# One run of column-half products per expert, then the scatter and both pairs of transposes

## The chip, the cores and the metric

The kernel runs on one core of a Trainium2 chip (trn2). The metric is the device time of one execution in microseconds; the number given for a kernel is the median of its runs.

## The reference

Two transformer layers over 256 tokens of width 1024. Layer 0 mixes with a gated linear attention, layer 1 with a differential attention; each is followed by a hierarchical mixture of experts, and the change touches only that mixture, which runs once per layer:

```python
def hier_moe(x, w_group, b_group, w_router, b_router, w_gate, w_up, w_down):
    ...                                  # a group, then 2 of its 4 experts for each token
    for e in range(MOE_EXPERTS):         # 16
        hdn = jax.nn.silu(t @ w_gate[e]) * (t @ w_up[e])      # 1024 -> 512
        y = y + combine[:, e:e + 1] * (hdn @ w_down[e])       # 512 -> 1024
    return y.reshape(B, S, D)
```

All arithmetic is float32.

## The kernel before

Each token takes two experts, so an expert sees about 32 of the 256 tokens. The kernel gives each expert 64 places. It gathers the tokens of four experts at a time into `xg` by products with one-hot matrices (line 548), and adds an expert's result back by a product with the transposed one-hot matrix `st`, which is called the scatter (line 664). Experts with more than 64 tokens get a further block; layer 1 always runs one such block as a 17th pass of the loop, so the two loops together have 33 passes.

With 64 tokens a product fills only half of the columns of TensorE's array. So the products with the weights are issued as pairs, one on each column half, that run at the same time; the profile marks them with the tile 128\*64. The gather, the scatter and the transposes use the whole array (128\*128). Of one expert:

- `gu_part` (line 604): tokens times gate and up weights, in four parts (0,), (1,), (2,) and (3,) with one weight tile each, on column halves, into a bank `pB`.
- `act_part`: ScalarE takes the silu of the gate half into `sl` (line 611), VectorE multiplies it with the up half into `hd` (line 613).
- `tr_part`: TensorE transposes `hd` in two pieces (line 620, whole array), VectorE copies the result to `ht` (line 623).
- `down_part`: `ht` times the down weights, on column halves (line 632). ScalarE and VectorE scale the result by the combine weights `wst` and split it in two numbers (lines 640 and 641).
- `s_prep`: VectorE builds the weighted one-hot matrix `ohw` (line 586), TensorE transposes it in two pieces (line 589, whole array), VectorE makes `st` of the result (line 591), and ScalarE sums the rows of the same bank into `wst` with its output thrown away into `jk` (line 594).
- `scatter`: four products on the whole array into the four banks of `y` (line 664).

The loop is pipelined by one expert: in the pass of expert e, the down products and the scatter are those of expert e - 1. Within a pass TensorE's order before is gu (0), transposes of `hd`, gu (1), down, transposes of `ohw`, gu (2, 3), scatter. Each engine works through its own queue in the order in which the scheduler of the kernel's framework put it. `issue_after` pins instructions of an engine behind a given one of the same engine.

The buffers `sl` and `jk` have the same tag with one buffer, so a silu and a row sum never hold it together:

```python
jk = mp.tile([128, S], F32, tag="sl", bufs=1, name=nm("jk"))   # s_prep, line 593
...
sl = mp.tile([128, fw], F32, tag="sl", bufs=1, name=nm("sl"))  # act_part, line 610
```

The weights (6 MB an expert) come through a ring of 16 tiles of 1 MB, filled by one DMA queue.

Of the kernel before, what the change touches and what calls it, by code (L numbers as in the profile page):

```python
# [22 lines left out]
E = 16  # L23
# [20 lines left out]
def body(ctx, tc, x, w_in, wa_out, kv_w, wq, wb_out, wg, wu, wd, gate2, rows, rtab, lng, lnb, cblob, pblob, onehot, out):  # L44
    nc = tc.nc
    pe, act, dve, pool, sp = nc.tensor, nc.scalar, nc.vector, nc.gpsimd, nc.sync
# [17 lines left out]
    def pB():  # L64
        return psum.tile([128, 512], F32, tag="B", bufs=2, name=nm("pB"))
# [14 lines left out]
    ident = ident_r.bitcast(F32)  # L80
# [383 lines left out]
    def moe(layer, M, lg, rstd, nd, fold, side=None):  # L464
        with tc.tile_pool(name=f"moe{layer}", bufs=1) as mp:
# [42 lines left out]
            OH = {}  # L508
# [73 lines left out]
            def s_prep(ohv, m, c_):  # L582

                w2 = mp.tile([128, 2, 2, m], F32, tag="ohw", bufs=2, name=nm("ohw"))
                for b in range(2):
                    dve.tensor_scalar(w2[:, b], ohv(b).unsqueeze(1).broadcast_to([128, 2, m]), c_[:, b:b + 1], None, op0=ALU.mult)
                p = pC()
                for b in range(2):
                    pe.transpose(p[0:2 * m, b * 128:b * 128 + 128], w2[:, b].rearrange("p d s -> p (d s)"), ident)  # L589
                st = mp.tile([128, S], F32R, tag="st", bufs=2, name=nm("st"))[0:2 * m]  # L590
                dve.tensor_scalar(st, p[0:2 * m, 0:256], 0.0, None, op0=ALU.is_gt)  # L591
                ws = sm([128, 1], "wst")
                jk = mp.tile([128, S], F32, tag="sl", bufs=1, name=nm("jk"))
                act.activation(jk[0:2 * m], p[0:2 * m, 0:256], AF.Copy, accum_out=ws[0:2 * m])
                return st, ws

            def gu_part(ws, js, xg, p, nt):
                m, fw = 128 // nt, FF // nt
# [17 lines left out]
            def tr_part(h, nt, filler=0):  # L616
                n = 4 // nt
                pt = pC()
                for c in range(n):
                    mm = pe.transpose(pt[:, c * 128:c * 128 + 128], h[:, c * 128:c * 128 + 128], ident)  # L620
                warm(filler, mm)
                ht = mp.tile([128, n, 128], F32, tag="ht", bufs=2, name=nm("ht"))
                dve.tensor_copy(ht, pt[:, 0:n * 128].rearrange("p (c t) -> p c t", c=n))  # L623
                return ht

            def down_part(wd_, ht, ws, nt, filler=0):

                m, n, w = 128 // nt, 4 // nt, D // nt
                p = [pB(), pC()]
                for q in range(4):  # L630
                    for c in range(nt):
                        mm = pe.matmul(p[2 * c // nt][c * m:c * m + m, 0:w], ht[:, q % n, (q // n) * m:(q // n) * m + m], wd_[q // 2][:, q % 2, c * w:c * w + w],  # L632
                                  start=q == 0, stop=q == 3)
                warm(filler, mm)
                o = [mp.tile([128, 512], F32R, tag="o", bufs=2, name=nm("o"))[0:2 * m] for _ in range(2)]
                for c in range(nt):
                    h, f = 2 * c // nt, slice(c * w % 512, c * w % 512 + w)
                    src, a = p[h][c * m:c * m + m, 0:w], h * m
                    hi, lo = o[h][a:a + m, f], o[h][m - a:2 * m - a, f]
                    act.activation(hi, src, AF.Copy, scale=ws[a:a + m, 0:1])  # L640
                    dve.scalar_tensor_tensor(lo, src, ws[a:a + m, 0:1], hi, op0=ALU.mult, op1=ALU.subtract)
                return o

            def down_last(wd_, ht, ws):

# [15 lines left out]
            def scatter(st, o, last, cols_first=False):  # L661
                for i in range(4):
                        b, c = (i % 2, i // 2) if cols_first else (i // 2, i % 2)
                        pe.matmul(y[b][c], st[:, b * 128:b * 128 + 128], o[c], start=False, stop=last, skip_group_check=True)  # L664

            def blocks():

# [62 lines left out]
            def overflow(left, base, rev):  # L730

                ei, q, cwx = pick(left, base, rev)
                ws, wdn = reload(ei, lambda j: spare_tile(1 + j % 2, [128, 2048], F32, nm("W")), pool, mybir.EngineType.Pool)
                oh = mp.tile([128, 2, 64], F32, tag="ohw", bufs=2, name=nm("ohx"))
                for b in range(2):
                    dve.tensor_scalar(oh[:, b], iota, q[:, b:b + 1], None, op0=ALU.is_equal)
                st, wsx = s_prep(lambda b: oh[:, b], 64, cwx)
                p = pC()
                pv = p.rearrange("p (k s) -> p k s", k=KC)
                for k in range(KC):  # L740
                    for b in range(2):
                        pe.matmul(pv[:, k], xa[:, b, k * 128:k * 128 + 128], oh[:, b], start=b == 0, stop=b == 1)
                xg = mp.tile([128, KC, 64], F32, tag="o", bufs=2, name=nm("xgx"))
                gv, bv = (pb[:, c:c + KC].unsqueeze(2).broadcast_to([128, KC, 64]) for c in (gcol, bcol))
                dve.tensor_mul(xg, pv, gv)
                dve.tensor_add(xg, xg, bv)
                p = pB()
                gu_part(ws, range(4), lambda k: xg[:, k], p, 2)
                ht = tr_part(act_part(p, 2), 2)
                scatter(st, down_part(wdn, ht, wsx, 2), True)  # L750

            xs0 = [split_x(k, dve) for k in range(4)]
            act.activation(sm([128, 2], "warm"), xs0[3][:, 0, 0, 0:2], AF.Exp, scale=0.0)
# [5 lines left out]
            for e in range(E + layer):  # L759
                g = min(e // 4, 3)  # L760
                if e in (4, 8, 12):
                    with after(held[e][1]):
                        one_hot(g)
                    gather_group(g, held[e][0])
                sl4 = slice((e - 4 * g) * 64, (e - 4 * g) * 64 + 64)
                xg = lambda k, t=xg_tiles[g if e < E else 4], s=sl4 if e < E else slice(0, 64): t[:, k, s]
                p = pB()
                mm = gu_part(M[e][0], (0,), xg, p, 2)
                if prev is not None:
                    with tc.issue_after(getattr(mm, "ins", mm)):  # L770
                        ht = tr_part(prev[0], 2)
                mm = gu_part(M[e][0], (1,), xg, p, 2)
                if prev is not None:
                    with tc.issue_after(getattr(mm, "ins", mm)):
                        o = down_part(M[e - 1][1], ht, prev[2], 2)
                sp_ = s_prep(lambda b: OH[g][:, b, e - 4 * g], 64, cw[:, :, e] if e < E else extra[2])
                gu_part(M[e][0], (2, 3), xg, p, 2)
                if prev is not None:
                    scatter(prev[1], o, False)
                h = act_part(p, 2)  # L780
                if e == 1:
                    over = blocks()
                    extra = over[1]
                    if layer:
                        M.append(reload(extra[0], lambda j: ring_slot(), sp, mybir.EngineType.SP))
                    nblocks = nc.values_load(over[0][0:1, 0:1], min_val=0, max_val=7, skip_runtime_bounds_check_because="512 tokens of experts, 65 or more for a block")
                prev = (h, *sp_)
                if e in (1, 5, 9):
                    held[e + 3] = anchor[0], anchor[1]
                if e == 5:  # L790
                    xr = spare_tile(2, [128, 2, D], F32, "xr")
                    for _ in residual(2 * layer, xr):
                        pass

                    for b in range(2):
                        for h in range(2):
                            v = xr[:, b, h * 512:h * 512 + 512]
                            hi, lo = (mp.tile([128, 512], F32R, tag="o", bufs=2, name=nm("res")) for _ in range(2))
                            act.activation(hi, v, AF.Copy)
                            dve.tensor_sub(lo, v, hi)  # L800
                            for a in (hi, lo):
                                pe.matmul(y[b][h], ident_r, a, start=False, stop=False, skip_group_check=True)
                if e == 9 and layer:
                    gb = spare_tile(0, [128, 2, 2, 512], F32, "gb")
                    for i in range(2):
                        for h in range(2):
                            act.activation(gb[:, i, h], bcast_row(8 * i + 4 * layer + 2 + h, pC), AF.Copy)
                if e == 9 and side:
                    side()
            o = down_last(M[-1][1], tr_part(prev[0], 2), prev[2])  # L810
            scatter(prev[1], o, True, True)
            with tc.If(nblocks > 0, label=f"over{layer}"):
                with tc.For_i(0, nblocks, 1):
# [163 lines left out]
    prev = None  # L977
# [231 lines left out]
```

## Time and profile before

| | us |
|---|---|
| median of 3 runs (780.3 to 781.99) | 780.58 |
| the profiled execution, its own time | 782.23 |
| the profiled execution, span from first to last instruction | 780.6 |
| TensorE busy in the span | 751.2 |

The span is what the trace shows; the profiled execution's own time is 1.6 us more, and is itself 1.65 us above the median. In a trace, a product of a 32-bit operand appears as two matmul records, so `gu_part` of one weight tile, 4 products, is 8 records. The granted TensorE clock is given as a share of full speed: 1.00 is 2.4 GHz and 0.50 is 1.2 GHz.

### The profile page before, as it was taken

To read this page: it belongs to the slowest core of one execution; us is meant where nothing else is said; L and a number is where in the kernel's file an instruction comes from. 1 tells how busy PE (TensorE), PEld (TensorE's weight loads), DVE (VectorE), ACT (ScalarE), POOL (GpSimd) and SP (SyncE) were. 2 spreads that over 40 slices of the span, in tenths; PEclk is the share of its full clock that TensorE was granted. 3 is DMA by queue.
4 is the path that set the end of the run, shared out by engine and by line. 5 is a ranking of instruction groups with operands and counts; after the bars stand their busy time and mean duration, and the time that the engine had idled before them with its cause. 6 is when DMAs were issued, how large, how long until landed. Compare 5 with 4: busy or idle time off the path is not lost. (4 is left out here: it accounts for less than half of the span.)

```text
span 780.6 us, 10650 instructions
## 1 busy us (share of the span) xinstructions
PE 751.2 (96%) x3762; PEld 404.2 (52%) x3762; DVE 362.7 (46%) x959; ACT 299.7 (38%) x655; POOL 8.4 (1%) x20
## 2 busy tenths in 40 slices
PE   7999999999999999999899999999999999999993
PEld 5887677534333433433689887763343243343331
DVE  3645576533363422422567777773344432332225
ACT  4444466523222331312557666562132232242123
POOL 1100000000000000000000000000000000000000
PEclk9999999999999999999999999999999999999997
DMA  7999448499999999999998336619999999999941
GB/s 217 312 385 392 168 164 295 152 381 397 394 386 393 392 395 396 393 392 367 290 363 314 144 111 215 216 56 370 393 395 395 394 391 390 397 394 392 391 168 56
DMA packets 131792, 246.02 MB, mean 315 GB/s; under 512 B 7916, under 2 KB 38101, under 8 KB 131734
## 3 DMA queue, kind: packets, MB, share of 16 engines
q1 hardware_dynamic: 131270, 244.68, 86.3%
q8 instruction: 32, 0.52, 0.3%
q10 hardware_dynamic: 432, 0.59, 0.2%
q14 instruction: 26, 0.21, 0.1%
q0 software_dynamic: 32, 0.01, 0.0%
HBM read 244.19 MB, written 1.06 MB: 314 GB/s over the span
## 5 line engine op out<-in xcount | busy, mean ns | idle before, releaser
L604 PE MATMUL pB<-W,xg 128*64 128x512 f32 x1056 | 258.7, 602 | 0.0
L604 PEld LDWEIGHTS pB<-W,xg 128*64 128x64 f32 x1056 | 69.1, 136 | 117.1 <-issue 110.2
L632 PE MATMUL pC<-W,ht 128*64 128x512 f32 x248 | 112.9, 594 | 0.0
L632 PE MATMUL pB<-W,ht 128*64 128x512 f32 x248 | 112.9, 594 | 0.0
L640 ACT ACTIVATE o<-pB,wst 64x512 fp32r<-64x512 f32 x31 | 21.1, 682 | 221.8 <-PE pC L632 208.4
L591 DVE TENSOR_SCALAR st<-pC 128x256 fp32r<-128x256 f32 x33 | 14.0, 425 | 155.2 <-PE pC L589 155.2
L119 DVE TENSOR_TENSOR lo<-W,hi 128x512 fp32r<-128x512 f32 x96 | 66.3, 696 | 39.9 <-PE pA L128 26.4
L118 ACT ACTIVATE hi<-W 128x512 fp32r<-128x512 f32 x96 | 59.5, 630 | 51.4 <-PE pA L129 29.8
L632 PEld LDWEIGHTS pB<-W,ht 128*64 128x64 f32 x248 | 33.3, 137 | 62.8 <-issue 61.2
L664 PE MATMUL pA<-o,st 128*128 128x512 f32 x132 | 40.2, 423 | 2.7 <-DVE o L658 2.1
L623 DVE COPY ht<-pC 128x256 f32<-128x256 f32 x33 | 14.0, 424 | 60.8 <-PE pC L620 60.7
L613 DVE TENSOR_TENSOR hd<-sl,pB 128x256 f32<-128x256 f32 x33 | 13.9, 422 | 56.7 <-ACT sl L611 56.6
L548 PE MATMUL pC<-OH,xs 128*128 128x256 f32 (+1 forms) x256 | 36.4, 292 | 3.1 <-ACT xg L555 1.9
L664 PEld LDWEIGHTS pA<-o,st 128*128 128x128 f32 x132 | 21.9, 188 | 33.5 <-issue 23.5
L548 PEld LDWEIGHTS pC<-OH,xs 128*128 128x128 f32 x256 | 32.8, 190 | 10.9 <-ACT xs L529 6.1
L127 PE MATMUL pA<-x1Thi,hi 128*128 128x256 f32 x128 | 36.5, 288 | 0.0
L632 PEld LDWEIGHTS pC<-W,ht 128*64 128x64 f32 x248 | 33.3, 137 | 6.1 <-issue 5.1
L128 PE MATMUL pA<-x1Tlo,hi 128*128 128x256 f32 x128 | 36.2, 285 | 0.0
L129 PE MATMUL pA<-x1Thi,lo 128*128 128x256 f32 x128 | 35.6, 288 | 0.0
L611 ACT ACTIVATE sl<-pB 128x256 f32<-128x256 f32 x33 | 12.7, 385 | 58.6 <-PE pB L604 58.4
L128 PE MATMUL pA<-lo,xThi 128*128 128x384 f32 (+1 forms) x96 | 35.0, 364 | 0.0
L129 PE MATMUL pA<-hi,xTlo 128*128 128x384 f32 (+1 forms) x96 | 34.7, 361 | 0.0
(340 smaller groups left out, 1148.1 us busy)
## 6 DMA issues: line engine op xcount, KB each, us to landing
W<-in_moe_w_gate_dram SPq DMA_DIRECT2D x132, 512.0 KB, 10.9
W<-in_moe_w_up_dram SPq DMA_DIRECT2D x132, 512.0 KB, 10.8
W<-in_moe_w_down_dram SPq DMA_DIRECT2D x66, 1024.0 KB, 12.0
W<-in_a_w_in_dram SPq DMA_DIRECT2D x16, 256.0 KB, 6.3
W<-in_a_w_in_dram SPq DMA_DIRECT2D x4, 1024.0 KB, 13.3
W<-in_a_w_out_dram SPq DMA_DIRECT2D x4, 1024.0 KB, 14.9
W<-in_kv_w_dram SPq DMA_DIRECT2D x4, 1024.0 KB, 8.9
W<-in_b_w_q_dram SPq DMA_DIRECT2D x16, 256.0 KB, 5.4
```

The lines of the kernel that those rows point to most:

```text
L118: act.activation(hi, src, AF.Copy)
L119: dve.tensor_sub(lo, src, hi)
L127: pe.matmul(o, l[0], r[0], start=first, stop=False, skip_group_check=skip)
L128: pe.matmul(o, l[0], r[1], start=False, stop=False, skip_group_check=skip)
L129: pe.matmul(o, l[1], r[0], start=False, stop=last, skip_group_check=skip)
L548: pe.matmul(o, xs[k][:, q // 2, q % 2], OH[g][:, q % 2].rearrange("p e s -> p (e s)"), start=q == 0, stop=q == 3)
L591: dve.tensor_scalar(st, p[0:2 * m, 0:256], 0.0, None, op0=ALU.is_gt)
L604: mm = pe.matmul(p[c * m:c * m + m, 0:2 * fw].rearrange("p (g f) -> p g f", g=2), xg(k), w[:, :, kk, c * fw:c * fw + fw], start=k == 0, st ...
L623: dve.tensor_copy(ht, pt[:, 0:n * 128].rearrange("p (c t) -> p c t", c=n))
L632: mm = pe.matmul(p[2 * c // nt][c * m:c * m + m, 0:w], ht[:, q % n, (q // n) * m:(q // n) * m + m], wd_[q // 2][:, q % 2, c * w:c * w + w] ...
L640: act.activation(hi, src, AF.Copy, scale=ws[a:a + m, 0:1])
L664: pe.matmul(y[b][c], st[:, b * 128:b * 128 + 128], o[c], start=False, stop=last, skip_group_check=True)
```

## The change

A pass now has on TensorE: gu (0), down products of expert e - 1, gu (1, 2, 3), scatter of expert e - 1, transposes of `ohw` of expert e, transposes of `hd` of expert e. All column-half products of a pass form one run, and all whole-array work stands behind it. The transposes of `hd` thereby move from the pass of e + 1 to the end of the pass of e. Chains of `issue_after` pin this order on TensorE. Nothing is computed differently.

```diff
                 p = pB()
-                mm = gu_part(M[e][0], (0,), xg, p, 2)
-                if prev is not None:
-                    with tc.issue_after(getattr(mm, "ins", mm)):
-                        ht = tr_part(prev[0], 2)
-                mm = gu_part(M[e][0], (1,), xg, p, 2)
+                with after(prev and prev[4]):
+                    mm = gu_part(M[e][0], (0,), xg, p, 2)
                 if prev is not None:
-                    with tc.issue_after(getattr(mm, "ins", mm)):
-                        o = down_part(M[e - 1][1], ht, prev[2], 2)
-                sp_ = s_prep(lambda b: OH[g][:, b, e - 4 * g], 64, cw[:, :, e] if e < E else extra[2])
-                gu_part(M[e][0], (2, 3), xg, p, 2)
-                if prev is not None:
-                    scatter(prev[1], o, False)
-                h = act_part(p, 2)
+                    with after(mm):
+                        o, mm = down_part(M[e - 1][1], ht, prev[2], 2)
+                with after(mm):
+                    mm = gu_part(M[e][0], (1, 2, 3), xg, p, 2)
+                with after(mm):
+                    if prev is not None:
+                        mm = scatter(prev[1], o, False)
+                    with after(mm):
+                        sp_ = s_prep(lambda b: OH[g][:, b, e - 4 * g], 64, cw[:, :, e] if e < E else extra[2])
+                    h = act_part(p, 2)
+                    with after(sp_[2]):
+                        ht, mm = tr_part(h, 2)
...
-                prev = (h, *sp_)
+                prev = (h, *sp_, mm)
...
-            o = down_last(M[-1][1], tr_part(prev[0], 2), prev[2])
+            o = down_last(M[-1][1], ht, prev[2])
```

The other lines of the diff only hand the last TensorE instruction of `s_prep`, `tr_part`, `down_part` and `scatter` back to the caller.

TensorE's queue before, in the pass of expert 2 of layer 0 (down products, of which 2 of 8 rows are shown, and the scatter are expert 1's; `W` is a weight tile, `hd_1878` expert 1's, `ohw_1932` expert 2's):

```order
L604 MATMUL pB_1902<-W_200,xg_1719 64x512 x4
L620 MATMUL pC_1907<-ident_r,hd_1878 128x128 x2
L604 MATMUL pB_1902<-W_203,xg_1719 64x512 x4
L632 MATMUL pB_1916<-W_196,ht_1910 64x512
L632 MATMUL pC_1917<-W_196,ht_1910 64x512
...
L589 MATMUL pC_1935<-ident_r,ohw_1932 128x128 x2
L604 MATMUL pB_1902<-W_206,xg_1719 64x512 x4
L604 MATMUL pB_1902<-W_209,xg_1719 64x512 x4
L664 MATMUL pA_1658<-o_1926,st_1859 128x512
```

TensorE's queue of the change in the same pass (`hd_1957` and `ohw_1944` are expert 2's):

```order
L604 MATMUL pB_1907<-W_200,xg_1719 64x512 x4
L632 MATMUL pB_1912<-W_196,ht_1883 64x512
L632 MATMUL pC_1913<-W_196,ht_1883 64x512
...
L604 MATMUL pB_1907<-W_203,xg_1719 64x512 x4
L604 MATMUL pB_1907<-W_206,xg_1719 64x512 x4
L604 MATMUL pB_1907<-W_209,xg_1719 64x512 x4
L664 MATMUL pA_1658<-o_1922,st_1871 128x512
...
L589 MATMUL pC_1947<-ident_r,ohw_1944 128x128 x2
L620 MATMUL pC_1959<-ident_r,hd_1957 128x128 x2
```

The transposes of `ohw` moved from before gu (2, 3) to behind the scatter, and the transposes of `hd` directly behind them; 31 of the 33 passes have these neighbours, and the first pass of each layer, which has no scatter, has line 589 and line 620 behind its gu (3).

ScalarE's queue before, in the passes of experts 2 and 3 of layer 0 (lines 640: results of the down products; `jk`: row sum; `sl`: silu):

```order
L640 ACTIVATE o_1926<-pB_1916,wst_1861 64x512
L640 ACTIVATE o_1927<-pC_1917,wst_1861 64x512
L594 ACTIVATE jk_1941,wst_1940<-pC_1935 128x256
L611 ACTIVATE sl_1955<-pB_1902 128x256
L640 ACTIVATE o_1983<-pB_1973,wst_1940 64x512
```

ScalarE's queue of the change at the same place:

```order
L640 ACTIVATE o_1922<-pB_1912,wst_1873 64x512
L640 ACTIVATE o_1923<-pC_1913,wst_1873 64x512
L594 ACTIVATE jk_1953,wst_1952<-pC_1947 128x256
L611 ACTIVATE sl_1955<-pB_1907 128x256
L640 ACTIVATE o_1979<-pB_1969,wst_1952 64x512
```

Nothing moved on ScalarE: the row sum of expert 2 (line 594) stands ahead of its silu (line 611) both times. What changed is the place on TensorE of the transposes `pC_1935` or `pC_1947` that the row sum reads.

## Rows read from the trace of the kernel before

**Rows 1.** The page's busy times: engine, busy us (share of span), instructions.
```profile
PE 751.2 (96%) x3762; PEld 404.2 (52%) x3762; DVE 362.7 (46%) x959; ACT 299.7 (38%) x655; POOL 8.4 (1%) x20
```

**Rows 2.** TensorE's waits: us in total, times, longest us (longest wait for weights).
```profile
PEld pB L604 <- DMA W<-in_moe_w_gate_dram: 2.9, 9, 0.8
```

**Rows 3.** Timeline of TensorE, one pass of layer 1: start us, us, instruction.
```profile
552.17 3.65 PE L604 MATMUL pB<-W,xg 128*64 128x512 f32 x16
555.76 1.20 PE L664 MATMUL pA<-o,st 128*128 128x512 f32 x4
556.88 1.94 PE L604 MATMUL pB<-W,xg 128*64 128x512 f32 x8
558.75 0.44 PE L620 MATMUL pC<-ident_r,hd 128*128 128x128 f32 x2
559.12 1.94 PE L604 MATMUL pB<-W,xg 128*64 128x512 f32 x8
560.88 0.59 PE L632 MATMUL pB<-W,ht 128*64 128x512 f32 x1
...
564.42 0.44 PE L589 MATMUL pC<-ident_r,ohw 128*128 128x128 f32 x2
564.79 3.65 PE L604 MATMUL pB<-W,xg 128*64 128x512 f32 x16
```

**Rows 4.** Timeline of TensorE: a scatter followed by whole-array products.
```profile
191.87 1.20 PE L664 MATMUL pA<-o,st 128*128 128x512 f32 x4
192.91 2.06 PE L548 MATMUL pC<-OH,xs 128*128 128x256 f32 x16
```

**Rows 5.** Timeline, layer 0: the first transposes of `ohw` and what follows.
```profile
151.24 0.44 PE L589 MATMUL pC<-ident_r,ohw 128*128 128x128 f32 x2
151.72 0.42 DVE L591 TENSOR_SCALAR st<-pC 128x256 fp32r<-128x256 f32 x1 [1.08 <-PE pC L589]
152.18 0.38 ACT L594 ACTIVATE jk<-pC 128x256 f32<-128x256 f32 x1 [2.38 <-DVE st L591]
152.46 0.19 ACT L594 ACTIVATION_READ_ACCUMULATOR jk<-pC 128x1 f32 x1
```

**Rows 6.** Timeline: the one pass where silu follows the row sum at once.
```profile
241.59 0.38 ACT L594 ACTIVATE jk<-pC 128x256 f32<-128x256 f32 x1
...
242.22 0.39 ACT L611 ACTIVATE sl<-pB 128x256 f32<-128x256 f32 x1
```

**Rows 7.** Timeline: the end of layer 1's loop, from its last scatter in the loop.
```profile
760.81 1.20 PE L664 MATMUL pA<-o,st 128*128 128x512 f32 x4
760.99 0.39 ACT L611 ACTIVATE sl<-pB 128x256 f32<-128x256 f32 x1 [2.01 <-PE pB L604]
761.41 0.42 DVE L613 TENSOR_TENSOR hd<-sl,pB 128x256 f32<-128x256 f32 x1 [2.08 <-ACT sl L611]
761.88 0.44 PE L620 MATMUL pC<-ident_r,hd 128*128 128x128 f32 x2
...
762.84 0.43 PE L652 MATMUL pB<-W,ht 128*64 128x256 f32 x1 [0.52 <-DVE ht L623]
```

**Rows 8.** Line 611: duration ns min/median/max, first and last start us.
```profile
L611 ACT ACT_TABLE_LOAD  x2: 1283/1283/1283, 155.4 to 531.9; - x2
```

**Rows 9.** Windows: us; busy us (count) by engine; granted clock, DMA share, GB/s.
```profile
29.30:33.00 3.70, 3.70 (x22) 2.67 (x20) 2.56 (x9) 1.82 (x4) 1.45 (x2) 1.00 1.14 317
33.00:36.40 3.40, 3.40 (x12) 2.94 (x11) 2.20 (x5) 0.63 (x1) 0.00 (x0) 0.50 1.14 319
...
376.00:380.00 4.00, 2.84 (x11) 2.04 (x12) 2.72 (x5) 3.55 (x7) 0.31 (x2) 1.00 1.17 298
766.00:770.00 4.00, 1.76 (x10) 0.65 (x6) 2.19 (x5) 3.09 (x6) 0.00 (x0) 1.00 0.02 6
770.00:772.00 2.00, 0.00 (x0) 0.00 (x0) 1.93 (x6) 1.34 (x5) 0.00 (x0) 0.56 0.00 0
```

**Rows 10.** Timeline of TensorE: one product of the stretch before 33.00.
```profile
30.64 0.38 PE L398 MATMUL pB<-ls,ones 1*128 1x1 f32 x2
```

More of the change, by code (lines that the diff above doesn't have):

```diff
@@ L588, in s_prep @@
                 for b in range(2):
-                    pe.transpose(p[0:2 * m, b * 128:b * 128 + 128], w2[:, b].rearrange("p d s -> p (d s)"), ident)
+                    mm = pe.transpose(p[0:2 * m, b * 128:b * 128 + 128], w2[:, b].rearrange("p d s -> p (d s)"), ident)
                 st = mp.tile([128, S], F32R, tag="st", bufs=2, name=nm("st"))[0:2 * m]
@@ L594, in s_prep @@
                 act.activation(jk[0:2 * m], p[0:2 * m, 0:256], AF.Copy, accum_out=ws[0:2 * m])
-                return st, ws
+                return st, ws, mm
             def gu_part(ws, js, xg, p, nt):
@@ L623, in tr_part @@
                 dve.tensor_copy(ht, pt[:, 0:n * 128].rearrange("p (c t) -> p c t", c=n))
-                return ht
+                return ht, mm
             def down_part(wd_, ht, ws, nt, filler=0):
@@ L641, in down_part @@
                     dve.scalar_tensor_tensor(lo, src, ws[a:a + m, 0:1], hi, op0=ALU.mult, op1=ALU.subtract)
-                return o
+                return o, mm
             def down_last(wd_, ht, ws):
@@ L663, in scatter @@
                         b, c = (i % 2, i // 2) if cols_first else (i // 2, i % 2)
-                        pe.matmul(y[b][c], st[:, b * 128:b * 128 + 128], o[c], start=False, stop=last, skip_group_check=True)
+                        mm = pe.matmul(y[b][c], st[:, b * 128:b * 128 + 128], o[c], start=False, stop=last, skip_group_check=True)
+                return mm
             def blocks():
@@ L736, in overflow @@
                     dve.tensor_scalar(oh[:, b], iota, q[:, b:b + 1], None, op0=ALU.is_equal)
-                st, wsx = s_prep(lambda b: oh[:, b], 64, cwx)
+                st, wsx, _ = s_prep(lambda b: oh[:, b], 64, cwx)
                 p = pC()
@@ L748, in overflow @@
                 gu_part(ws, range(4), lambda k: xg[:, k], p, 2)
-                ht = tr_part(act_part(p, 2), 2)
-                scatter(st, down_part(wdn, ht, wsx, 2), True)
+                ht, _ = tr_part(act_part(p, 2), 2)
+                scatter(st, down_part(wdn, ht, wsx, 2)[0], True)
             xs0 = [split_x(k, dve) for k in range(4)]
```

## The prediction

> **What bounds the kernel now.** I read the page first: TensorE is busy for 751.2 of 780.6 us [rows 1]. Then its waits: the largest wait for weights in the expert loop is 2.9 us in 9 pieces [rows 2], so the loop runs at TensorE's pace and not at the pace of the weights. Then the timeline of one pass [rows 3]. The reader should see that the starts follow each other without a hole and that one pass is 564.79 - 552.17 = 12.62 us long. What ScalarE and VectorE do in a pass lies beside this, because TensorE always has the products of another part to do. So two questions decide: how long TensorE's own work gets, and whether it still has something to do while the other engines work.
>
> **What becomes shorter.** TensorE's times of a pass come from starts in [rows 3].
> - 16 records of line 604 take 555.76 - 552.17 = 3.59 us up to the scatter, 8 take 558.75 - 556.88 = 1.87 up to the transposes. Eight more records cost 1.72, and the rest, 0.15, is paid where the array goes from column halves to whole.
> - 8 records of line 604 ahead of the down products take 560.88 - 559.12 = 1.76.
> - In the change the run is gu (0), 1.76, the 16 records of the down products, 2 x 1.72 = 3.44, and 24 records of gu (1, 2, 3), 3.59 + 1.72 = 5.31: together 10.51 us.
> - The scatter takes 1.04 when whole-array work follows [rows 4], and 556.88 - 555.76 = 1.12 when column halves follow [rows 3].
> - The transposes of `hd` and the way back to column halves take 559.12 - 558.75 = 0.37.
>
> So without any wait a pass takes 10.51 + 1.04 + x + 0.37 = 11.92 + x, where x is the time from the start of the transposes of `ohw` to the start of those of `hd`. TensorE's own work in x is no more than the 0.37 that the two transposes take today with their way back (564.79 - 564.42); none of today's rows has them without it, so x lies between 0 and 0.37 if nothing waits, and I take 0.2: 12.12 us, 0.50 less than today.
>
> **The skill's rule on this.** The rows show a price for each way in or out of column halves, 0.08 to 0.15 us where it can be taken apart as above. The Trainium skill, page "TensorEngine Tiling (Array Packing)", section "Tiling Modes", Key Properties, states that a change of the tiling mode drains TensorE. By that rule alone the change, which makes one visit to the whole array out of three, should make the kernel faster; the first rival below is this case.
>
> **What becomes longer.** The transposes of `hd` are behind those of `ohw` now, directly. They need `hd`, hence the silu. On ScalarE the silu stands behind the row sum of `ohw`, in both kernels (the order of ScalarE ahead of this text), and the two also share one buffer (tag `sl`, one buffer), so it could not pass anyway. Before, this cost nothing: the transposes of `ohw` came 3.59 us of gu (2, 3) ahead of the silu's input. Now the row sum's input is made only after the scatter, so the chain below starts when TensorE has nothing left in the pass but the transposes that wait for it:
> 1. Transposes of `ohw` to VectorE's `st`: 151.72 - 151.24 = 0.48 [rows 5].
> 2. `st` to the row sum, which waits for it since both read one bank (its row names `st` L591 as releaser): 152.18 - 151.72 = 0.46 [rows 5].
> 3. Row sum to silu: at least 152.46 + 0.19 - 152.18 = 0.47, the end of its accumulator read [rows 5]; 242.22 - 241.59 = 0.63 in the one pass where the silu followed at once [rows 6]. I take 0.55, the middle, since ScalarE will be idle ahead of it as in the first, but the silu's start is seen in the second only.
> 4. Silu to the transposes of `hd`, with VectorE's product between: 761.88 - 760.99 = 0.89 [rows 7].
>
> So x = 0.48 + 0.46 + 0.55 + 0.89 = 2.38 us (2.30 to 2.46), of which TensorE works some 0.2 and stands for 2.2. A pass is 11.92 + 2.38 = 14.30 us, **1.68 longer** than today (1.60 to 1.76). For 33 passes that is 55.4 us (52.8 to 58.1). The last pass of each layer gains some 0.3 less, and the passes with gathers and the residual are taken to keep their extra time; I leave both in the range.
>
> In each layer the first silu has a table load of 1.283 us ahead of it [rows 8]. Today TensorE covers it with the gu records of experts 0 and 1; in the change it stands in the chain behind the row sum: 2 x 1.28 = 2.6 us.
>
> Costed at nothing: `ht`, which the down products need 762.84 - 761.88 = 0.96 after the start of the transposes [rows 7], is covered by 0.37 + 1.76 of transposes and gu (0). The scaled result of the down products is covered by 5.31 us of gu (1, 2, 3). The weight tile of gu (1) goes back to the ring 3.44 us of down products later; what hides that is that each pass gets longer while the weights come no slower, and if the cover were gone it could cost the 2.9 us of [rows 2] again.
>
> **The clock.** From 29.30 to 33.00 TensorE is shown busy throughout, but with products as small as the single column of [rows 10]; then it runs at 0.50, the 1.2 GHz level, for 3.40 us, and it is back at 1.00 after that [rows 9]. At half speed 3.40 us do the work of 1.7, so one such fall costs about 1.7 us. At the end of the kernel it fell soon after 770.00, behind a stretch of 4.00 us with 1.76 busy; a stretch of 4.00 us with 2.84 busy at 376.00 left it at 1.00 [rows 9]. Four microseconds around the new stall have at most 4.00 - 2.2 = 1.8 busy, so the stall looks like the stretch that fell. It comes in every pass, 2.2 us in 14.30. But since neither row is this case, I don't put a fall behind each: the bounds are no fall and 33 falls (56 us), and I take 12, about a third, as nothing tells how often such a stretch is enough: 12 x 1.7 = 20.4 us.
>
> **Sum.** Against the profiled execution's own time, 782.23 us: 782.2 + 55.4 + 2.6 + 20.4 = 860.6. That execution was 1.65 us above the median of the runs, so I forecast **859 us** for the median. Without falls of the clock the same sum gives 838.6.
>
> **Rivals.**
> - *No stall, faster.* The silu gets through right after gu (3). For it: at the end of the loop today `hd` is ready for its transposes 1.07 us after the scatter starts (761.88 - 760.81) [rows 7], just when the scatter is through. The pass is then 12.12 us, and 33 x 0.50 = 16.5 makes the median 764. Against it: ScalarE's order and the single buffer. The point that decides is x = 12.62 - 11.92 = 0.70 us: whatever lets the transposes of `hd` start within 0.70 us of those of `ohw` makes the change a gain. The first two links of my chain alone are 0.94.
> - *Stall, clock stays.* 839 us. For it: the clock stayed at 1.00 through the stretch at 376.00 with its idle pieces, and 1.8 busy is only an upper bound near the 1.76 of the one that fell.
> - *Stall, clock falls behind nearly every one.* 33 x 1.7 = 56 in place of 20: 895 us. For it: the comparison with the stretch at 766.00. Against it: the stretch at 376.00 had two idle pieces and did not fall, and between the stalls TensorE runs for 12 us without a hole.
>
> **Chances.** Stall with some falls 0.64; stall with none or a few 0.20; falls nearly everywhere 0.08; no stall 0.05; the rest, 0.03, is a shorter chain that comes out level. The range reaches down to the case without falls with the low bound of the chain, 782.2 - 1.65 + 52.8 + 2.6 = 836, with 4 us off for the passes that gain less: 832. It reaches up to 58.1 of chain and 24 falls, 780.6 + 58.1 + 2.6 + 40.8 = 882. About 0.2% is what a measurement of this kernel can tell from no change; by the cases, faster 0.06, same 0.02, slower 0.92.
>
> **What would show it.** Right: passes of about 14.3 us at full clock; the transposes on line 620 idle for about 2.2 us ahead of them, released by `hd` of line 613; the silu of line 611 released by ScalarE's own row sum and no longer by TensorE; windows inside the loop with a granted clock under 1.00. The gain is seen as a run of 24 pairs without a break, some 10.5 us from the first gu record to the scatter. Wrong: line 620 starting 0.2 us behind line 589; or a row sum that doesn't wait for `st`, which would take 0.46 out of each pass, 15 us in all; or a clock of 1.00 throughout.

## The result and the profile after

| | before | after |
|---|---|---|
| median, us (4 runs each) | 780.86 (780.3 to 781.99) | 879.74 (875.54 to 882.5) |
| the profiled execution, own time, us | 782.23 | 878.96 |
| its span, us | 780.6 | 877.3 |
| its mean granted clock | 0.991 | 0.950 |

The ratio is 1.126, with an interval of 1.1212 to 1.1308: the change costs 98.9 us, where 78 were forecast. The first view is the page: its busy times, which answer to [rows 1], and one of its groups (busy us, mean ns, idle time of the engine before it and what ended that).

```profile
PE 778.2 (89%) x3762; PEld 422.1 (48%) x3762; DVE 362.9 (41%) x959; ACT 300.3 (34%) x655; POOL 8.4 (1%) x20
...
L620 PE MATMUL pC<-ident_r,hd 128*128 128x128 f32 x66 | 15.2, 314 | 70.7 <-DVE hd L613 67.5
```

TensorE has the same 3762 instructions, but 99.1 us of the span are idle where it was 29.4. Of these 70.7 stand ahead of line 620, the transposes of `hd`. And the same instructions are busy for 27.0 us longer, although the run of column-half products saves time; this points to the clock (below). The view of TensorE's waits puts 67.5 us in 32 pieces on `hd`, and one more of 3.2 us, in the first pass of layer 1, on a weight tile by name:

```profile
PE pC L620 <- DVE hd L613: 67.5, 32, 3.2
...
PE pC L620 <- DMA W<-in_moe_w_up_dram: 3.2, 1, 3.2
```

That tile was not what ended the last one: the timeline has `hd` (line 613) from 582.83 to 583.25 there and the transposes at 583.31, 0.06 us behind it, just as in the plain pass below. So all 33 waits, 70.7 us, are for `hd`.

The timeline of all engines has the first pass of layer 0 and then a plain pass, which is one without a gather, the residual or other extra work (start us, us, instruction, idle time before it). Only the products of lines 604 and 632 appear as two records each; a transpose or a product of the scatter is one.

```profile
155.03 0.44 PE L589 MATMUL pC<-ident_r,ohw 128*128 128x128 f32 x2
...
156.25 0.20 ACT L594 ACTIVATION_READ_ACCUMULATOR jk<-pC 128x1 f32 x1
156.46 1.28 ACT L611 ACT_TABLE_LOAD   x1
157.76 0.39 ACT L611 ACTIVATE sl<-pB 128x256 f32<-128x256 f32 x1
...
158.65 0.69 PE L620 MATMUL pC<-ident_r,hd 128*128 128x128 f32 x2 [3.18 <-DVE hd L613]
...
187.23 1.19 PE L664 MATMUL pA<-o,st 128*128 128x512 f32 x4
188.26 0.38 PE L589 MATMUL pC<-ident_r,ohw 128*128 128x128 f32 x2
188.68 0.42 DVE L591 TENSOR_SCALAR st<-pC 128x256 fp32r<-128x256 f32 x1 [4.25 <-PE pC L589]
189.20 0.38 ACT L594 ACTIVATE jk<-pC 128x256 f32<-128x256 f32 x1 [5.62 <-DVE st L591]
189.59 0.20 ACT L594 ACTIVATION_READ_ACCUMULATOR jk<-pC 128x1 f32 x1
189.83 0.38 ACT L611 ACTIVATE sl<-pB 128x256 f32<-128x256 f32 x1
190.24 0.42 DVE L613 TENSOR_TENSOR hd<-sl,pB 128x256 f32<-128x256 f32 x1 [0.63 <-ACT sl L611]
190.72 0.44 PE L620 MATMUL pC<-ident_r,hd 128*128 128x128 f32 x2 [2.08 <-DVE hd L613]
191.09 1.94 PE L604 MATMUL pB<-W,xg 128*64 128x512 f32 x8
...
196.29 5.32 PE L604 MATMUL pB<-W,xg 128*64 128x512 f32 x24
201.54 1.20 PE L664 MATMUL pA<-o,st 128*128 128x512 f32 x4
```

Read the plain pass from 188.26 to 190.72: TensorE's transposes, `st` on VectorE, row sum and silu on ScalarE, `hd` on VectorE, one behind the other, while TensorE stands. Of the engines' other work only VectorE's `ohw` for the next pass lies beside them, 0.48 us from 189.13, and it is over before `hd` begins. The scatter starts are 201.54 - 187.23 = 14.31 us apart, where [rows 3] had 12.62. The gain is there too: the run of column-half products takes 201.54 - 191.09 = 10.45 us without a break.

The windows show the clock (us; busy us by engine; granted clock, DMA share, GB/s): the stall of one pass, the 3.40 us behind it, the stall of the next pass and the 3.40 us behind that, and a long stretch of layer 0.

```profile
172.60:175.60 3.00, 1.01 (x8) 0.70 (x10) 2.34 (x9) 2.19 (x7) 0.00 (x0) 1.00 1.04 386
175.60:179.00 3.40, 3.40 (x12) 1.04 (x10) 1.65 (x9) 0.00 (x0) 0.00 (x0) 0.52 1.06 402
...
189.00:191.00 2.00, 0.28 (x2) 0.20 (x2) 1.01 (x4) 0.97 (x3) 0.00 (x0) 1.00 1.05 389
191.00:194.40 3.40, 3.40 (x18) 1.21 (x18) 0.42 (x1) 0.00 (x0) 0.00 (x0) 1.00 1.06 395
160.00:300.00 140.00, 124.67 (x520) 49.05 (x517) 44.91 (x104) 30.29 (x65) 0.00 (x0) 0.91 0.87 322
```

Two stalls of the same 2.08 us: behind the first TensorE runs at 0.52 for 3.40 us, behind the second at 1.00. A fall is here such a stretch at half clock. In windows of 0.2 us the two expert loops show 19 of them, each beginning between 0.3 us before the end of a stall and 2.1 us behind it; 16 are 3.4 us long and 3 are 6.8, together 22 times 3.4. Before, there was none in the loops, only the stretch of [rows 9] at 33.00, which is still there, and the end of the kernel.

The time that the clock takes can also be read from the whole span, as span times one minus the mean clock: 877.3 x 0.050 = 43.9 us now, 780.6 x 0.009 = 7.0 before. The difference, 36.9 us, is the clock's part of the 96.7 us between the spans; 59.8 are left for the chain. A plain pass with a fall takes 238.41 - 222.41 = 16.00 us where one without takes 14.31, 1.69 more; 22 times 1.7 us give 37.4. The Trainium skill, page "TensorE: Matmul & The Clock Gate", section "Terms", prices throttled time as that time times the missing share of the clock; the trace agrees, since half of 3.40 us is 1.70.

### The profile page after: what moved, and what is told of

It reads as the page before. It is cut to its first block, busy times and chain, and to the rows that moved or that the text cites. A ratio compares the mean times of both kernels' runs of the same rounds, so it can differ in the third digit from the quotient of the medians.

```text
span 877.3 us, 10603 instructions
## 1 busy us (share of the span) xinstructions
PE 778.2 (89%) x3762; PEld 422.1 (48%) x3762; DVE 362.9 (41%) x959; ACT 300.3 (34%) x655; POOL 8.4 (1%) x20
## 5 line engine op out<-in xcount | busy, mean ns | idle before, releaser
L604 PE MATMUL pB<-W,xg 128*64 128x512 f32 x1056 | 284.1, 633 | 0.0
L604 PEld LDWEIGHTS pB<-W,xg 128*64 128x64 f32 x1056 | 78.6, 142 | 139.1 <-issue 135.4
L632 PE MATMUL pB<-W,ht 128*64 128x512 f32 x248 | 121.1, 631 | 0.0
L632 PE MATMUL pC<-W,ht 128*64 128x512 f32 x248 | 115.9, 611 | 0.0
L641 DVE SCALAR_TENSOR_TENSOR o<-pB,wst,o 64x512 fp32r<-64x512 f32 x31 | 23.1, 744 | 173.0 <-ACT o L640 173.0
L620 PE MATMUL pC<-ident_r,hd 128*128 128x128 f32 x66 | 15.2, 314 | 70.7 <-DVE hd L613 67.5
L118 ACT ACTIVATE hi<-W 128x512 fp32r<-128x512 f32 x96 | 59.5, 630 | 51.3 <-PE pA L129 29.7
L594 ACT ACTIVATE jk<-pC 128x256 f32<-128x256 f32 x33 | 12.7, 384 | 184.4 <-DVE st L591 184.4
L632 PEld LDWEIGHTS pB<-W,ht 128*64 128x64 f32 x248 | 36.0, 149 | 61.1 <-issue 60.2
L620 PEld LDWEIGHTS pC<-ident_r,hd 128*128 128x128 f32 x66 | 6.9, 146 | 78.5 <-DVE hd L613 78.5
L548 PE MATMUL pC<-OH,xs 128*128 128x256 f32 (+1 forms) x256 | 40.8, 312 | 1.3 <-ACT xs L529 0.6
## 6 DMA issues: line engine op xcount, KB each, us to landing
W<-in_a_w_in_dram SPq DMA_DIRECT2D x4, 1024.0 KB, 12.8
```

What stands on the lines that cost most here:

```text
L118: act.activation(hi, src, AF.Copy)
L548: pe.matmul(o, xs[k][:, q // 2, q % 2], OH[g][:, q % 2].rearrange("p e s -> p (e s)"), start=q == 0, stop=q == 3)
L604: mm = pe.matmul(p[c * m:c * m + m, 0:2 * fw].rearrange("p (g f) -> p g f", g=2), xg(k), w[:, :, kk, c * fw:c * fw + fw], start=k == 0, st ...
```

## Experiments

The theory was: ScalarE's row sum stands ahead of the silu, its input is now made last in the pass, so a chain through three engines lies open, and its idle time lets the clock fall. The rivals were that the shared buffer is the cause by itself, that falls are not due to the stall, and that the gain of fewer visits to the whole array can be had in full (764 us). Ratios are against runs of the kernel before on the same chip.

**The stall filled.** Nine products of zeros keep TensorE busy while it waits; the chain is as in the change. The zeros are added to the banks of `y`, so nothing of the computation changes. (A line is added further up as well, so line 589 is 590 in its profile, and so on.)

```diff
-                    with after(sp_[2]):
+                    with after(warm(9, sp_[2])):
                         ht, mm = tr_part(h, 2)
```

> The change with 9 products of zeros (some 2.05 us, whole array, added to y) between the transposes of ohw and those of hd, so that TensorE is busy through the stall without using the time. Theory (the stall costs twice, once as time and once through the clock): same passes of 14.3 us, clock 1.00 in the loop, 780.9 + 55.4 + 2.6 = 839 us; the rest of the change's 879.7, some 40 us, was the clock. Rival (the chain itself is longer than 1.68 us per pass in many passes, and the clock costs only the 20 us predicted): about 859 us.

Measured: 841.28 us, ratio 1.0761 (1.0743 to 1.0779), span 839.4, mean clock 0.994. The timeline of TensorE, and a window to compare with the last one above:

```profile
182.66 1.20 PE L665 MATMUL pA<-o,st 128*128 128x512 f32 x4
183.69 0.38 PE L590 MATMUL pC<-ident_r,ohw 128*128 128x128 f32 x2
183.83 2.21 PE L181 MATMUL pA<-zero_r 128*128 128x512 f32 x9
186.15 0.44 PE L621 MATMUL pC<-ident_r,hd 128*128 128x128 f32 x2
```

```profile
160.00:300.00 140.00, 138.33 (x638) 62.34 (x636) 47.98 (x111) 32.49 (x70) 0.00 (x0) 1.00 0.97 360
```

The transposes of `hd` still come 186.15 - 183.69 = 2.46 us behind those of `ohw`, so the chain is untouched, but the clock is at 1.00. The chain alone costs 7.6%, some 59.5 us (forecast: 58.0), and the falls are due to TensorE's idle time in the stall: 879.74 - 841.28 = 38.5 us between two medians.

**The stall half filled.** The same with 4 products.

```diff
-                    with after(warm(9, sp_[2])):
+                    with after(warm(4, sp_[2])):
```

> The change with 4 products of zeros in the stall in place of 9; the zeros are added to no result. The chain is the same, so a plain pass without a fall still takes 14.3 us, and some 1.1 us of the 2.1 stay idle. If the number of falls depends on how much of the hole is left (my theory): far fewer than the change's 20, some 2 to 6, 843 to 850 us. Rival: any hole in every pass brings the falls, whatever its length: 15 to 20 of them, 865 to 880 us.

Measured: 846.12 us, ratio 1.082 (1.0804 to 1.0835), mean clock 0.987. The timeline of TensorE:

```profile
200.67 0.38 PE L590 MATMUL pC<-ident_r,ohw 128*128 128x128 f32 x2
200.81 1.12 PE L181 MATMUL pA<-zero_r 128*128 128x512 f32 x4
203.13 0.44 PE L621 MATMUL pC<-ident_r,hd 128*128 128x128 f32 x2 [1.21 <-DVE hd L614]
```

The distance is 2.46 us again, of which 1.21 are idle. Only two falls lie in the loops, one of them behind the stall of layer 0's first pass, of which 2.30 us stay idle, and one behind the last pass of layer 0. So it matters how much of the hole stays idle, not only that there is one.

**The row sum ahead of `st`, the stall filled.** This takes link 2 of the prediction's chain out. It has 7 products of zeros (that line is not shown).

```diff
-                dve.tensor_scalar(st, p[0:2 * m, 0:256], 0.0, None, op0=ALU.is_gt)
                 ...
                 act.activation(jk[0:2 * m], p[0:2 * m, 0:256], AF.Copy, accum_out=ws[0:2 * m])
+                dve.tensor_scalar(st, p[0:2 * m, 0:256], 0.0, None, op0=ALU.is_gt)
```

> The change with products of zeros in the stall (7 in place of 9), and the row sum written ahead of st, so that it reads the bank first. The zeros are added to no result. If links 2 and 3 of the chain are what the prediction says, the row sum starts 0.46 us earlier and the plain pass takes 14.31 - 0.46 = 13.85 us; 33 x 0.46 = 15.2 less than with the zeros alone, 841.3 - 15.2 = 826 us, clock 0.99. Rival: the wait for st is not a link (the row sum is held by something else, or st becomes what the pass waits for): 14.3 us and 841.

Measured: 825.02 us, ratio 1.0565 (1.0548 to 1.0582), plain passes 13.79 and 13.85. The timeline of all engines:

```profile
182.13 0.38 PE L590 MATMUL pC<-ident_r,ohw 128*128 128x128 f32 x2
...
182.54 0.39 ACT L594 ACTIVATE jk<-pC 128x256 f32<-128x256 f32 x1 [5.11 <-PE pC L590]
...
183.18 0.38 ACT L612 ACTIVATE sl<-pB 128x256 f32<-128x256 f32 x1
...
183.59 0.42 DVE L614 TENSOR_TENSOR hd<-sl,pB 128x256 f32<-128x256 f32 x1
184.07 0.44 PE L621 MATMUL pC<-ident_r,hd 128*128 128x128 f32 x2
```

The row sum's releaser is now TensorE, and the distance is 184.07 - 182.13 = 1.94 us, 0.52 less. So the wait for `st` is a link of the chain, as the prediction has it, and the time fell to 825 us where 826 were forecast.

**Silu ahead of the row sum, in two ways.** First `jk` gets a buffer of its own; the scheduler then places the silu ahead by itself.

```diff
-                jk = mp.tile([128, S], F32, tag="sl", bufs=1, name=nm("jk"))
+                jk = mp.tile([128, S], F32, tag="jk", bufs=1, name=nm("jk"))
```

> The change with a buffer of its own for the thrown-away output of the row sum, nothing else; TensorE's order stays as in the change (scatter, ohw, hd), but the scheduler now puts the silu ahead of the row sum on ScalarE. Theory (the shared buffer put the silu behind the row sum): the transposes of hd start some 0.2 us behind those of ohw, passes of 12.1 us, about 764 us. Rival (the order on TensorE, ohw ahead of hd, is what costs): still passes of 14.3 us and falls of the clock, about 876 us.

Measured: 784.1 us, ratio 1.0038 (1.0023 to 1.0053): no stall of the plain passes, so the rival's 876 is refuted, but the 764 is missed by 20 us. Second, the buffer stays shared, and the silu is only written ahead of `s_prep`.

```diff
+                    h = act_part(p, 2)
                     with after(mm):
                         sp_ = s_prep(...)
-                    h = act_part(p, 2)
```

> The order of TensorE and the shared buffer stay as in the change; only the silu is written ahead of s_prep, so that ScalarE has silu, then row sum. If the order of ScalarE's queue is what costs (my theory): the silu waits for gu (3) alone, hd is ready when the scatter is through, a plain pass takes 12.0 us, the clock stays above 0.98, 782 to 785 us. If the sharing of the one buffer costs something of its own, whatever the order: the row sum now waits for hd to be read before it can write, and the down products' scale comes late; then a pass above 12.6 us and above 790 us.

Measured: 784.56 us, ratio 1.0047 (1.0031 to 1.0063), as forecast. The timeline of all engines:

```profile
191.79 0.38 ACT L611 ACTIVATE sl<-pB 128x256 f32<-128x256 f32 x1 [3.72 <-PE pB L604]
192.21 0.42 DVE L613 TENSOR_TENSOR hd<-sl,pB 128x256 f32<-128x256 f32 x1 [3.27 <-ACT sl L611]
...
192.72 0.38 PE L589 MATMUL pC<-ident_r,ohw 128*128 128x128 f32 x2
...
192.94 0.38 PE L620 MATMUL pC<-ident_r,hd 128*128 128x128 f32 x2
...
193.66 0.38 ACT L594 ACTIVATE jk<-pC 128x256 f32<-128x256 f32 x1 [1.48 <-DVE st L591]
```

The silu waits for TensorE's gu (line 604) alone, and the transposes of `hd` start 192.94 - 192.72 = 0.22 us behind those of `ohw`. Both variants have plain passes of 12.0 us. Whether the buffer is shared makes no difference here; the order does. The buffer has a part in how the order came about, since in the first variant nothing but the buffer is changed and the scheduler then puts the silu ahead. What keeps both above 764 lies in the passes with extra work: the pass with the residual takes 22.2 us (20.1 before), those with a gather 0.3 to 0.7 us longer than before (17.99 for 17.67 in one), and the loops have two or three falls.

**Own buffer, the silu pinned behind the row sum.** The fourth case: a buffer of its own, but the order of the change.

```diff
-                jk = mp.tile([128, S], F32, tag="sl", bufs=1, name=nm("jk"))
-                act.activation(jk[0:2 * m], ...)
+                jk = mp.tile([128, S], F32, tag="jk", bufs=1, name=nm("jk"))
+                anchor[0] = act.activation(jk[0:2 * m], ...)
...
-                    h = act_part(p, 2)
+                    with after(anchor[0]):
+                        h = act_part(p, 2)
```

> jk has a buffer of its own, and the silu is pinned behind the row sum on ScalarE, as it stands in the change. If the place in ScalarE's queue is the cause (my theory): as the change, plain passes of 14.3 us, falls of the clock, 875 to 882 us. Rival, the shared buffer is the cause by itself: the passes take 12.0 us and the time is 784.

Measured: 863.34 us (856.88 to 869.43), ratio 1.1037 (1.097 to 1.1104): the rival's 784 is refuted, and the theory's 875 is missed by 12. The timeline says where these are:

```profile
187.45 0.20 ACT L594 ACTIVATION_READ_ACCUMULATOR jk<-pC 128x1 f32 x1
187.56 0.36 ACT L611 ACTIVATE sl<-pB 128x256 f32<-128x256 f32 x1
187.95 0.42 DVE L613 TENSOR_TENSOR hd<-sl,pB 128x256 f32<-128x256 f32 x1 [0.42 <-ACT sl L611]
188.43 0.44 PE L620 MATMUL pC<-ident_r,hd 128*128 128x128 f32 x2 [1.88 <-DVE hd L613]
```

The silu starts 0.11 us after the start of the accumulator read; with the shared buffer it was 189.83 - 189.59 = 0.24, after its end. Plain passes take 14.11 us, 0.20 less, or 6.6 us over 33; 0.13 of the 0.20 is this earlier start. The idle time of 1.88 us in place of 2.08 also means fewer falls: span times one minus the clock is 864.5 x 0.043 = 37.2 us, 6.7 less than in the change. Together that is 13.3, and the spans differ by 12.8. So the order on ScalarE is the cause, and the buffer has a small price of its own once the order is that one.

**The transposes of `hd` ahead of those of `ohw`.** The silu then has nothing in front of it on ScalarE or TensorE.

```diff
-                    with after(mm):
-                        sp_ = s_prep(...)
                     h = act_part(p, 2)
-                    with after(sp_[2]):
+                    with after(mm):
                         ht, mm = tr_part(h, 2)
+                    with after(mm):
+                        sp_ = s_prep(...)
+                    mm = sp_[2]
```

> The change with the two pairs of transposes behind the scatter swapped: first those of hd, then those of ohw (the silu is then traced ahead of the row sum). Theory (the change loses because the silu waits for the row sum of ohw; the single run of column-half products is itself a gain): no stall, passes of 12.1 us, 780.9 - 16.5 = about 764 us, clock 1.00 in the loop. Rival (the whole-array work behind one long run has to wait for hd anyway, whoever stands first): the transposes of hd stall at their new place too, passes over 13 us, more than 800 us.

Measured: 781.71 us (777.07 to 781.83, 10 runs), ratio 0.9984 (0.9969 to 1.0). Plain passes take 12.04 us, 0.57 less than before, and yet the 764 is missed. The time of a run goes with its mean clock, from 777.1 us at 0.992 to 781.8 at 0.985, which is two or three falls more or less. The profile, of the run of 777.07, says where the rest of the 16.5 us went. Its waits of TensorE, and the start of a pass with a gather in its timeline:

```profile
PE pA L664 <- DVE o L641: 2.6, 2, 1.3
...
PE pC L620 <- DVE hd L613: 1.9, 2, 0.9
PE pC L548 <- DVE ht L623: 1.8, 6, 0.3
```

```profile
192.05 0.42 PE L620 MATMUL pC<-ident_r,hd 128*128 128x128 f32 x2
192.31 0.38 PE L589 MATMUL pC<-ident_r,ohw 128*128 128x128 f32 x2
192.99 2.24 PE L548 MATMUL pC<-OH,xs 128*128 128x256 f32 x16 [0.30 <-DVE ht L623]
```

Only 15 of the 33 passes are plain, 15 x 0.57 = 8.6 us, and two more gain 1.5 each. The six passes with gathers take as long as before or up to 0.4 us more (17.67 and 17.69 for example): the gather needs a bank `pC`, and waits 0.30 us for the copy of `ht` out of it. That is about half of what a plain pass gains; the other half I have not taken apart. In the first pass of each layer the transposes of `hd` wait 0.9 us for the silu behind its table load; from the first gu record to the first scatter TensorE takes 22.60 us where it took 21.96. The pass behind that scatter is 0.63 longer too: a whole-array product that counts the tokens of the experts, which stood right behind the scatter before, now stands between two pieces of gu (0). What its place costs I have not taken apart. In the pass of each layer in which the residual is added the scatter waits 1.3 us for the scaled down products, and the pass is 0.86 longer. Before, other work of TensorE lay over these waits. One pass of layer 1 also has a fall that it had not; in return this execution lacks the stretch at half clock that stood at 33.00.

**Two visits to the whole array.** The transposes of `ohw` go back between the down products and gu (1), those of `hd` stay behind the scatter.

```diff
                 with after(mm):
+                    sp_ = s_prep(...)
+                with after(sp_[2]):
                     mm = gu_part(M[e][0], (1, 2, 3), xg, p, 2)
                 with after(mm):
                     if prev is not None:
                         mm = scatter(prev[1], o, False)
-                    with after(mm):
-                        sp_ = s_prep(...)
                     h = act_part(p, 2)
-                    with after(sp_[2]):
+                    with after(mm):
                         ht, mm = tr_part(h, 2)
```

> Half of the change: the transposes of ohw go back to their place of before (behind the down products), while those of hd stay behind the scatter. The row sum is then 5 us ahead of the silu again. Theory: no stall, two visits to the whole array in place of three; a pass of 1.76 + 3.54 + 0.37 + 5.31 + 1.07 + 0.37 = 12.42 us, 0.20 less than before, 780.9 - 6.6 = 774 us. Rival (any hd transposes directly behind the scatter stall): slower than before.

Measured: 786.77 us, ratio 1.0056 (1.0037 to 1.0075). Plain passes take 12.41 us, between the 12.04 with one visit and the 12.61 with three. The forecast of 774 is missed by 13 us, mostly in the two first passes, where the transposes of `hd` wait 2.3 us for the silu behind its table load:

```profile
PE pC L620 <- DVE hd L613: 4.6, 2, 2.3
```

A fall follows each of these two waits, and up to the first scatter of a layer TensorE takes 4.9 us longer than before. The pass with the residual is 1.0 longer in each layer.

**The lost passes as before.** The variant with `hd` first, but for some experts the transposes of `hd` stand one gu part into the next pass again. (The lines that are not shown leave gu (1) out behind the down products of such a pass and keep the order of the variant with `hd` first.)

```diff
+                    if late_:
+                        with after(mm):
+                            ht, mm = tr_part(prev[0], 2)
+                        with after(mm):
+                            mm = gu_part(M[e][0], (1,), xg, p, 2)
...
+                    late_ = e in (0, 3, 5, 7, 9, 11)
+                    if not late_:
+                        with after(mm):
+                            ht, mm = tr_part(h, 2)
```

> The order of the variant with the transposes of hd ahead of those of ohw, but for experts 0, 3, 5, 7, 9 and 11 the transposes of hd stand one gu part into the next pass, as in the kernel before. These are the passes (first silu, gathers, residual) in which the variant's 0.57 us a pass was lost in new waits. If those waits are where the gain went: some 3 us less than that variant, 774 us (span 772). Rival: the loss in these passes is TensorE's own work or the weights, and moves elsewhere: 777 to 782 as before.

Measured: 776.99 us, ratio 0.9946 (0.9932 to 0.996). The 774 was missed: the gather passes became 0.3 to 0.4 us longer (17.69 to 17.98 in one), since the gather now waits for the row sum to read its bank, as its waits of TensorE show:

```profile
PE pC L548 <- ACT jk L594: 2.6, 6, 0.6
```

Only experts 0 and 5 gained: 0.7 us up to the first scatter of each layer, and 0.3 in each pass behind the residual, though the pass with the residual itself got 0.2 longer (20.95 to 21.16 in layer 0). So the next variant does it for these two alone:

```diff
-                    late_ = e in (0, 3, 5, 7, 9, 11)
+                    late_ = e in (0, 5)
```

> As the mixed variant, but only experts 0 and 5 have their transposes of hd one gu part into the next pass; experts 3, 7, 9 and 11, whose passes got 0.2 to 0.4 us longer by it, have them behind the scatter again. If each pass keeps its own time: 7 passes of about 0.3 us come back, 777.0 - 2.1 = 775 us. Rival: what a gather pass gives back is lost in the next wait, and the time stays at 777.

Measured: 774.89 us (774.0 to 778.34, 6 runs), ratio 0.9919 (0.9903 to 0.9935). The forecast of 775 is met, and runs of the same mean clock, 0.991, differ by as much (777.0 to 777.6 in the last variant, 774.8 to 775.3 in this one). It beats both kernels, the one before by 0.8%. A plain pass in its timeline of TensorE:

```profile
341.34 1.20 PE L664 MATMUL pA<-o,st 128*128 128x512 f32 x4
342.37 0.42 PE L620 MATMUL pC<-ident_r,hd 128*128 128x128 f32 x2
342.63 0.38 PE L589 MATMUL pC<-ident_r,ohw 128*128 128x128 f32 x2
342.94 1.94 PE L604 MATMUL pB<-W,xg 128*64 128x512 f32 x8
...
353.39 1.20 PE L664 MATMUL pA<-o,st 128*128 128x512 f32 x4
```

## Why the prediction was right, and where it was off

- **Mechanism.** Right, and shown by the four cases of order and buffer (880 and 863 us with the row sum first, 784 and 785 with the silu first): passes of 14.31 us (forecast 14.30), line 620 idle for 2.08 us (2.2) with `hd` as releaser, the silu right behind ScalarE's own row sum. One step of the argument was wrong without harm to the number: the shared buffer does not forbid the silu to pass, as the run that writes the silu first shows.
- **The links.** 0.42, 0.52, 0.63 and 0.89 us in the plain pass above, 2.46 together, where 2.38 was taken. Link 3 was taken as 0.55, the middle of two rows; it was the upper one, [rows 6]. The accumulator read starts 0.39 us behind the row sum here (0.28 in [rows 5]), and with the shared buffer the silu starts behind its end, 0.24 later; with a buffer of its own it starts 0.11 later.
- **What gets shorter.** The run takes 10.45 us (10.51), and the x without a wait, 0.2 by choice, is 0.22 in the run with the silu written first, whose order on TensorE is that of the change.
- **Chain over the whole kernel.** 55.4 + 2.6 = 58.0 forecast; 59.5 by the filled stall, 59.8 by the profile. The table load in the first pass is there: x is 158.65 - 155.03 = 3.62 us, 1.16 more than in a plain pass, where 1.28 was taken.
- **The clock.** This term was mis-sized. "About a third" of the stalls, 12 falls, was a choice without a row behind it; the loops have 22 stretches of 3.4 us, so 37 to 39 us in place of 20.4. The size of one, 1.7 us, was right. The forecast of 859 lies 21 us below the measured time, of which 16 to 18 are this term and 1.5 to 2 the chain. That the measured 879.74 still lies in the range is owed to its upper end of 882, which goes by 24 falls, a number as freely chosen as the 12; one of the four runs, 882.5, lies above it.
- **The rivals.** *No stall* fell with the order on ScalarE. Its own sum was wrong too: 33 x 0.50 took every pass for a plain one, and without the stall the change's order on TensorE comes out at 784.1 to 784.6 us, the one with `hd` first at 781.7, and 774.9 at best. In the plain passes the gain is there, 12.61 - 12.04 = 0.57 us for two visits less. The Trainium skill, page "TensorEngine Tiling (Array Packing)", section "Tiling Modes", Key Properties, states that a change of the tiling mode drains TensorE; the trace agrees in sign, and no run here parts the drain from the rest of a visit. *Stall, clock stays* gave 839, and that kernel, with the stall filled, measured 841. *Falls nearly everywhere* needed 33; there were 19, of which three were of double length.
- **Costed at nothing.** `ht`, `o` and the ring of weights stayed hidden in the plain passes; TensorE's waits name `ht` only behind the end of each layer's loop, and the one of 3.2 us in the loops that goes by the name of a weight tile ended with `hd`, as said above.

What stays open: why 19 of 33 stalls are followed by a fall and 14 are not. The length does not tell them apart: 16 of the 19 and 13 of the 14 are of 2.08 us, and the 3.17 us in the first pass of layer 1 are followed by none. Nor does the program alone, since its four runs differ. Whether it matters when a stall comes was not tested. Also open are the 1.5 to 2 us by which the chain is longer than forecast.

## What to carry to other kernels

Gathering one engine's similar work into a run also gathers what is left, and what is left may be links of one chain: before moving a step to the end of a pass, follow its readers through the queues of the other engines. A step off the critical path (here a row sum of 0.38 us) can hold up a whole pass when its input is made late and something urgent stands behind it in the same engine's queue. And a gain per pass is only worth its number of plain passes: count those with extra work apart, because old covers are missing there.

## What was not expected of the hardware

A hole of about 2.1 us in a pass of 14.3, with TensorE busy otherwise, was enough for the half clock: a mean of 0.91 from 160 to 300 us, in stretches of 3.4 us or twice that. With 1.88 us of idle time the mean clock of the span was 0.957, with 1.21 it was 0.987, and without it 0.994, so that products of zeros, which shorten no chain, were worth 38.5 us. And the fall isn't sure: 14 of the 33 stalls had none behind them, and the same kernel's runs differ by 7 us (875.54 to 882.5 at 0.954 to 0.947).
